# Two heads' inverses stacked on their rows, and the right sides of a chunk made block-diagonal

## The chip, the core and the metric

The kernel runs on one core of one Trainium2 chip. The metric is the device time of one execution in microseconds; three executions of the kernel before took 3189.84 to 3195.04 us, with a median of 3192.13 us. The core has five engines that run their own instruction streams and wait for each other through semaphores: TensorE (PE, with its weight loads shown as PEld), VectorE (DVE), ScalarE (ACT), GpSimd (POOL) and SyncE (SP), which issues the DMAs.

## What is computed

One layer of a hybrid decoder, for a prompt of 2048 tokens and for 8 short sequences of 4 tokens each: a root-mean-square norm, one wide projection, a gated short convolution, an RWKV-7 branch of 16 heads of 64 channels, two output projections merged by gates, one more projection, and a final norm. The change lies in the RWKV-7 recurrence:

```python
def _rwkv7_scan(S0, r, k, v, decay, kk, a):
    def step(S, inp):
        r_t, k_t, v_t, d_t, kk_t, a_t = inp
        sa = jnp.einsum('bhvk,bhk->bhv', S, -kk_t)
        S = (S * d_t[:, :, None, :] + sa[..., None] * (kk_t * a_t)[:, :, None, :]
             + v_t[..., None] * k_t[:, :, None, :])
        y = jnp.einsum('bhvk,bhk->bhv', S, r_t)
        return S, y
```

## The kernel before

**Tiles and stages.** The prompt is cut into four sets of 512 tokens. For each set the first phase projects the normalised rows: every block of 128 output columns is a run of 24 matmuls of 128x512 into a PSUM tile `ip`, eight slices of the contraction by three products of high and low parts (`whl` are the weights, XH and XL the rows). Among these, PE gets the small matmuls of the RWKV branch. The last set is longer by the 32 tokens of the short sequences. A second phase does the output projections; the change does not touch it.

**The recurrence in chunks.** Heads are handled in pairs, eight pairs to a set, each pair on 128 partitions (head 0 on 0 to 63, head 1 on 64 to 127). A set has eight chunks of 64 tokens. Inside a chunk the recurrence is a unit lower triangular system. `rwkv_solve` and `rwkv_merge` invert it for all chunks of a pair ahead of time: DVE inverts 32x32 blocks, ACT copies them from `Xo` into `Xbd` (lines 986 to 988), and two rounds of 32x32 matmuls fill in the off-diagonal blocks. In `Xbd` each chunk has a block-diagonal 128x128 matrix, head 0's inverse at the upper left, head 1's at the lower right, zeros elsewhere.

**The chain.** `rwkv_chain` then goes through the eight chunks of a pair in order, since each needs the state S left by the one before:

1. PE multiplies S by the chunk's keys and receptances into PSUM (`pa`, line 1108).
2. DVE adds `P1` to the two 64x64 blocks of `pa`, giving the right sides `us`, head 0 on partitions 0 to 63, head 1 on 64 to 127, both in columns 0 to 63 (lines 1109 to 1111). ACT scales the state by the chunk's decay (`sp`, line 1113).
3. `inner` (lines 1067 to 1071): PE multiplies `us` by the chunk's matrix in `Xbd`, a 128x64 result in PSUM (`pb`). The next product needs both heads side by side on partitions 0 to 63 of SV. So DVE copies `pb`'s partitions 0 to 63 to SV's columns 0 to 63, and ACT copies `pb`'s partitions 64 to 127 to columns 64 to 127.
4. PE multiplies SV by `BKt` into the other half of `pb` (line 1118), and DVE updates S from it, one instruction per head (lines 1119 to 1121).

There are 4 sets x 8 pairs x 8 chunks = 256 such chunks. Every matmul on f32 tiles is two instructions (two passes) on PE, so the matmul of step 3 counts 512. The short sequences of the last set run through `inner` once per pair as well, from `rwkv_sequences`, with a matrix of their own in slot NCH of `Xbd` (line 1014).

**What sets the order.** The program is recorded once. The `ip` matmuls are the main stream; the RWKV steps are generators that hand control back at each `yield`. `Clock` keeps a planned time for each engine and each tile region, with a cost for each instruction in `Traced.cost` (for ACT 200 + 0.84 ns a column, for DVE 150 + 1.05 ns a column) and a lag of 60 ns to other engines, 200 ns behind PE. A generator goes on when the planned time of PE has reached the planned time at which the regions named in its last `yield` are ready (`Side.run`, line 329). So the planned costs set how many `ip` matmuls stand between two steps of the chain. On the chip each engine then runs its instructions in the recorded order, whatever their real times are.

`us` is a tile of a pool with two buffers (`sm`). `rst`, 1 within a chunk and 0 at its start, is an input of DVE's scan in `rwkv_keys` (line 851), one scan of 512 columns for a pair.

Of the kernel before, what the change touches and what calls it, by code (L numbers as in the profile page):

```python
# [7 lines left out]
F32 = mybir.dt.float32  # L8
F32R = mybir.dt.float32r
BF16 = mybir.dt.bfloat16  # L10
AF = mybir.ActivationFunctionType
ALU = mybir.AluOpType
# [4 lines left out]
P = 128  # L17
# [4 lines left out]
NCH = 8  # L22
NT = NCH * C
# [156 lines left out]
def hybrid_kernel(tc, x_prompt, x_sample, state_conv, state_shift, state_rwkv, norm_g, w_in, conv_w,  # L180
# [219 lines left out]
    con = ph1.enter_context(tc.tile_pool(name="con", bufs=1))  # L400
    xp = ph1.enter_context(tc.tile_pool(name="xp", bufs=1))
# [14 lines left out]
    BKt = xp.tile([P, NC1, P], F32, name="BKt")  # L416
    GMB = [xp.tile([P, NC1, 2, 2, C], F32, name=f"GM{i}") for i in range(2)]
    XB = [xp.tile([P, NC1, P], F32, name=f"Xbd{i}") for i in range(2)]
    SV = xp.tile([P, NC1, P], F32, name="SV")
    early = {}  # L420

# [65 lines left out]
                        base=0, channel_multiplier=1)  # L487
    V.transpose(X0.rearrange("p a b -> p (a b)"), xo0.rearrange("p a b c -> p (a b c)"))

    rst = con.tile([P, NT], F32, name="rst")  # L490
    V.memset(rst, 1.0)
    V.memset(rst.rearrange("p (c t) -> p c t", t=C)[:, :, 0:1], 0.0)
    rst_s = con.tile([P, NSAMP], F32, name="rst_s")
# [314 lines left out]
    def rwkv_keys(th, p, o):  # L808
# [116 lines left out]

        o.update(sz=sz, vT=vT, AR=AR, pe=pe, bv=bv)

    blk = [(slice(64 * h + 32 * b, 64 * h + 32 * b + 32)) for h in range(2) for b in range(2)]

    def rwkv_solve(th, p, o):  # L930
# [50 lines left out]
    def rwkv_merge(th, p, o):  # L981

        GM, Xo, Mo = (o[k] for k in ("GM", "Xo", "Mo"))
        Xbd = o["Xbd"] = XB[(th * NB + p) % 2]
        samp = th == LAST
        for i, g in enumerate(blk):
            A.copy(Xbd[g, 0:NCH, g].rearrange("p c (a e) -> p c a e", e=4),
                                                 Xo[g].rearrange("p a e c -> p c a e"))

        T11 = rw.tile([P, NCH, 32], F32, name="T11")  # L990
        for h in range(2):
            V.transpose(T11[blk[2 * h]], Xbd[blk[2 * h], 0:NCH, blk[2 * h]])
        yield W["bt"], [T11[0:96], Mo[64:96]], 1
        Wm = rw.tile([P, NCH, 32], F32, name="Wm")
        pt = new_pt([P, 512], F32, name="pt")
        for c in range(NCH):
            for h in range(2):
                T.matmul(pt[blk[2 * h + 1], c * 32:(c + 1) * 32], lhsT=Mo[64:96, c, :] if h else GM[0:32, c, 0, 0, 32:64],
                         rhs=T11[blk[2 * h], c, :], start=True, stop=True)
        for h in range(2):  # L1000
            A.copy(Wm[blk[2 * h + 1]], pt[blk[2 * h + 1], 0:NCH * 32].rearrange("p (c t) -> p c t", t=32))
        yield W["bt"], [Wm[32:128], Xbd[32:128]], 1
        pt = new_pt([P, 512], F32, name="pt")
        for c in range(NCH):
            for h in range(2):
                T.matmul(pt[blk[2 * h], c * 32:(c + 1) * 32], lhsT=Wm[blk[2 * h + 1], c, :],
                         rhs=Xbd[blk[2 * h + 1], c, blk[2 * h + 1]], start=True, stop=True)
        for h in range(2):
            A.copy(Xbd[blk[2 * h], 0:NCH, blk[2 * h + 1]],
                   pt[blk[2 * h], 0:NCH * 32].rearrange("p (c t) -> p c t", t=32))  # L1010
        yield W["bt"], (), samp
        if samp:
            for h in range(2):
                V.tensor_copy(Xbd[HS[h], NCH, HS[h]], GM[0:64, NCH, 0, h, :])

            M = Xbd[:, NCH, :]
            pt = new_pt([P, 512], F32, name="pt")
            T.transpose(pt[:, 0:P], M, ident)
            MT = sm.tile([P, P], F32, name="sq")
            A.copy(MT, pt[:, 0:P])  # L1020
            V.tensor_tensor(out=M, in0=M, in1=ident, op=ALU.add)
            yield W["samp"], [M, MT], 1
            for _ in range(SL - 2):
                pt = new_pt([P, 512], F32, name="pt")
                T.matmul(pt[:, 0:P], lhsT=MT, rhs=M, start=True, stop=True)
                V.tensor_tensor(out=M, in0=pt[:, 0:P], in1=ident, op=ALU.add)
                yield W["samp"], [M], 1
        yield W["merge"], [Xbd]
# [38 lines left out]
    def inner(c, pb, us, Xbd):  # L1067

        T.matmul(pb[:, 0:64], lhsT=Xbd[:, c, :], rhs=us, start=True, stop=True)
        V.tensor_copy(SV[0:64, c, 0:64], pb[0:64, 0:64])  # L1070
        A.copy(SV[0:64, c, 64:128], pb[64:128, 0:64])
# [19 lines left out]
    def rwkv_chain(th, p, o):  # L1091

        Yc = y_tile(th, o)
        AR, pe, GM, Xbd = (o[k] for k in ("AR", "pe", "GM", "Xbd"))
        samp = th == LAST
        S = St[p]

        P1 = rw.tile([P, NCH, 64], F32, name="P1")
        yield 0.0, (), 1 + samp
        A.copy(P1.rearrange("p c v -> p (c v)"), own_values(0, NCH, GM))  # L1100
        if samp:
            A.copy(Yc[:, NCH, :], own_values(NCH, 1, GM)[:, 0:64])
        yield W["gk"], [P1]
        for g in range(0, NCH, 4):
            pa = ps_a.tile([P, 4, P], F32, name="pa")
            for c in range(g, g + 4):
                PC = pe[:, c:c + 1]
                T.matmul(pa[:, c - g, :], lhsT=AR[:, c].rearrange("p q t -> p (q t)"), rhs=S, start=True, stop=True)
                us = sm.tile([P, 64], F32, name="us")
                for h in range(2):  # L1110
                    V.tensor_tensor(out=us[HS[h]], in0=pa[0:64, c - g, HS[h]], in1=P1[HS[h], c, :], op=ALU.add)
                sp = sm.tile([P, P], F32, name="sp")
                A.activation(out=sp, in_=S, func=AF.Copy, scale=PC)
                yield W["us"], [us]
                pb = ps_b.tile([P, 2, P], F32, name="pb")
                inner(c, pb[:, 0], us, Xbd)
                yield W["sa"], [SV[0:64, c, :]]
                T.matmul(pb[:, 1, :], lhsT=BKt[:, c, :], rhs=SV[:, c, :], start=True, stop=True)
                for h in range(2):
                    V.scalar_tensor_tensor(out=S[HS[h], HS[h]], in0=pb[HS[h], 1, HS[h]], scalar=PC[HS[h]], in1=sp[HS[h], HS[h]],  # L1120
                                           op0=ALU.mult, op1=ALU.add)
                yield W["state"], [S]
            for h in range(2):
                A.copy(Yc[HS[h], g:g + 4, :], pa[64:128, :, HS[h]])
        yield W["out"], [SV[0:64, 0:NCH]], 1 + samp
        all_rows(o, GM, Yc, samp)
        if samp:
            yield 0.0, (), 1
            pt = new_pt([P, 512], F32, name="pt")
            T.transpose(pt[:, 0:P], S, ident)  # L1130
            so = sm.tile([P, P], F32, name="sq")
            V.tensor_copy(so, pt[:, 0:P])
            for h in range(2):
                SP.dma_start(out=new_rwkv_p[0, 0, 2 * p + h], in_=so[HS[h], HS[h]])
# [261 lines left out]
    ncv = xp.tile([P, NB, 2 + 2 * NS], F32, name="ncv")  # L1396
    xsmp = xp.tile([P, NB, R], F32, name="xsmp")
    scv = xp.tile([P, NB, 2 * NS], F32, name="scv")
    for t in (BK[:, NCH], ARB[0][:, NCH], ARB[1][:, NCH], *XB):
        G.memset(t, 0.0)  # L1400

    def zero_rest():
# [220 lines left out]
```

## Time and profile before

| | |
|---|---|
| median of three executions | 3192.13 us (3189.84 to 3195.04) |
| profiled execution, its own time | 3193.32 us |
| profiled execution, its span from first to last instruction | 3191.6 us |
| mean granted clock of PE | 0.992 |
| DVE, SV<-pb 64x64, 256 copies | 209 ns each |
| ACT, SV<-pb 64x64, 256 copies | 208 ns each |
| first and last matmul pb<-us | 157.1 us and 2641.6 us |

A line of the profile names the engine, the line of the program (here nearly always L121, the helper that records every instruction, so the tile names tell the groups apart), the operation and its tiles as out<-in. In the list of groups come the shape, the count, the busy time in us and the mean length in ns, and behind the second bar the idle time of the engine just before these instructions and what ended it. In the list of waits stand the total in us, the number of times and the longest. In the timeline stand the start in us, the length, the instruction, and in brackets how long its engine had been idle before it. The ends of matmuls are modelled, and the next one starts before the modelled end of the last; distances from start to start are the safer reading.

### The profile page before, as it was taken

How to read it: one execution, taken by the hardware profiler on the slowest of the kernel's cores; microseconds unless marked ns; L12 is line 12 of the kernel's file. 1: busy time of each engine (PE TensorE's matmuls, PEld its weight loads, DVE VectorE, ACT ScalarE, POOL GpSimd, SP SyncE). 2: the span in 40 equal slices, each digit the busy share in tenths (PEclk: the TensorE clock that was granted, in tenths of full speed). 3: DMA queues.
4: the chain of work that ended last, by engine and by line, in shares of the span. 5: the costliest groups of instructions: out<-in, count | busy, mean ns of one | idle time of the engine just before them, and what ended most of it. 6: DMA issues, size and time to landing. Idle time of an engine off the chain costs nothing.

```text
span 3191.6 us, 55625 instructions
## 1 busy us (share of the span) xinstructions
PE 3092.0 (97%) x21530; PEld 2596.5 (81%) x21530; DVE 1992.5 (62%) x5704; ACT 1241.9 (39%) x2571; POOL 309.6 (10%) x517
## 2 busy tenths in 40 slices
PE   7999999999999999999999999999999999999998
PEld 6777777887777778877777789989889889778896
DVE  5687777776666666666666676766677664443332
ACT  5454445444333434434443334344444432211201
POOL 2011111111000001100101010000000000000000
PEclk9999999999999999999999999999999999999999
DMA  8786666644444444444444444434443469988863
GB/s 267 258 267 220 213 212 220 207 173 148 146 162 160 155 159 159 169 157 153 159 153 158 159 147 142 138 127 139 144 143 135 138 223 318 363 337 304 316 241 120
DMA packets 241504, 615.09 MB, mean 193 GB/s; under 512 B 33931, under 2 KB 143620, under 8 KB 187479
## 3 DMA queue, kind: packets, MB, share of 16 engines
q1 hardware_dynamic: 241094, 611.00, 55.8%
q8 instruction: 170, 2.79, 0.4%
q14 instruction: 96, 0.78, 0.1%
q0 software_dynamic: 144, 0.52, 0.0%
HBM read 452.10 MB, written 159.36 MB: 192 GB/s over the span
## 4 chain that ended last, share of the span: by engine, by line
PE 69%; DVE 18%; ACT 5%; issue 5%; DMA 3%; POOL 1%; SPq 0%; ACTq 0%; DVEq 0%; POOLq 0%
PE ip L121 49%; PE pt L121 10%; PE po L121 6%; PE pb L121 3%; DVE X L121 2%; DVE tmp L121 2%; DVE tt L121 2%; ACT tmp L121 2%; DVE Mi L121 2%; DVE whl L121 1%; DVE us L121 1%; PE pa L121 1%; DVE S L121 1%; DMA wraw<-in_w_in_dram 1%; ACT Xbd L121 1%
## 5 line engine op out<-in xcount | busy, mean ns | idle before, releaser
L121 PE MATMUL ip<-XH,whl 128*128 128x512 f32 (+3 forms) x7776 | 2105.1, 351 | 6.6 <-DVE gt L121 3.9
L121 PEld LDWEIGHTS ip<-XH,whl 128*128 128x128 f32 x7776 | 1342.0, 190 | 178.3 <-issue 27.5
L121 PE MATMUL ip<-XL,whl 128*128 128x512 f32 (+3 forms) x3888 | 1364.0, 351 | 2.7 <-POOL XL L121 2.6
L121 PEld LDWEIGHTS ip<-XL,whl 128*128 128x128 f32 x3888 | 738.5, 190 | 79.0 <-issue 7.0
L121 DVE TENSOR_TENSOR X<-X,tt 128x60 f32<-128x60 f32 (+24 forms) x992 | 211.7, 213 | 27.5
L121 DVE TENSOR_TENSOR tt<-Mi,X 128x60 f32<-128x60 f32 (+24 forms) x992 | 209.9, 212 | 27.4
L121 DVE SCALAR_TENSOR_TENSOR S<-pb,pe,sp 64x64 f32<-64x64 f32 x512 | 143.8, 281 | 106.6 <-PE pb L121 100.5
L121 ACT ACTIVATE sp<-S,pe 128x128 f32<-128x128 f32 x256 | 99.5, 400 | 244.7 <-DVE S L121 241.2
L121 ACT ACTIVATE tmp<-ip,vec 128x512 f32<-128x512 f32 (+2 forms) x174 | 103.2, 593 | 231.6 <-PE ip L121 230.2
L121 ACT COPY SV<-pb 64x64 f32<-64x64 f32 x256 | 53.3, 208 | 329.2 <-DVE SV L121 325.5
L121 DVE TENSOR_TENSOR whl<-wraw,whl 128x1024 fp32r<-128x1024 f32 x105 | 134.2, 1279 | 58.0 <-ACT whl L121 57.7
L121 PE MATMUL po<-whl,MH 128*128 128x512 f32 x544 | 170.4, 394 | 0.0
L121 DVE TENSOR_TENSOR us<-pa,P 64x64 f32<-64x64 f32 x512 | 110.2, 215 | 45.2 <-PE pa L121 33.7
L121 PEld LDWEIGHTS pb<-us,Xbd 128*128 128x128 f32 x512 | 85.9, 189 | 56.9 <-PE ip L121 21.5
L121 PE MATMUL ip<-RH,whl 128*128 128x512 f32 (+2 forms) x512 | 128.4, 341 | 1.7 <-DMA whl<-w_or 1.6
L121 PEld LDWEIGHTS pb<-SV,BKt 128*128 128x128 f32 x512 | 85.1, 189 | 54.6 <-ACT SV L121 45.9
L121 ACT CAST whl<-wraw 128x1024 fp32r<-128x1024 f32 x105 | 109.5, 1044 | 50.5 <-DMA wraw<-in_w_out_r_dram 14.8
L121 PE MATMUL pb<-SV,BKt 128*128 128x128 f32 x512 | 107.3, 291 | 17.4 <-ACT SV L121 17.3
L121 DVE TENSOR_TENSOR GM<-pt,mask_p 128x512 f32<-128x512 f32 x128 | 82.4, 685 | 64.4 <-PE pt L121 64.4
L121 PEld LDWEIGHTS po<-whl,MH 128*128 128x128 f32 x544 | 102.2, 188 | 24.0 <-DVE whl L121 0.3
L121 PE MATMUL pb<-us,Xbd 128*128 128x64 f32 x512 | 90.1, 258 | 23.7 <-DVE us L121 23.1
L121 ACT COPY Xbd<-Xo 32x256 f32<-32x256 f32 x128 | 88.1, 688 | 64.0 <-DVE Xo L121 61.9
(494 smaller groups left out, 3838.6 us busy)
## 6 DMA issues: line engine op xcount, KB each, us to landing
wraw<-in_w_in_dram SPq DMA_DIRECT2D x81, 512.0 KB
whl<-w_k SPq DMA_DIRECT2D x24, 1024.0 KB
whl<-w_r SPq DMA_DIRECT2D x24, 1024.0 KB
whl<-w_v SPq DMA_DIRECT2D x24, 1024.0 KB
whl<-w_z SPq DMA_DIRECT2D x24, 1024.0 KB
whl<-w_xin SPq DMA_DIRECT2D x24, 1024.0 KB
whl<-w_cg SPq DMA_DIRECT2D x24, 1024.0 KB
whl<-w_zc SPq DMA_DIRECT2D x24, 1024.0 KB
```

What stands on the lines that cost most here:

```text
L121: r = f(*a, **k)
```

## The change

The two inverses of a chunk are stacked in `Xbd`: both heads write their blocks to columns 0 to 63 (`col` takes the place of `blk` in the column index), head 0 on partitions 0 to 63, head 1 on 64 to 127; columns 64 to 127 of the eight chunks stay zero. The right sides go into a block-diagonal 128x128 tile `UB`, head 1 now in columns 64 to 127; two such tiles, cleared once, take turns. The product then has 128 columns instead of 64, and its partitions 0 to 63 hold both heads side by side, as SV needs them: one ACT copy of 64x128 takes the place of a DVE copy and an ACT copy of 64x64 each. `inner` stays for the short sequences. `rst` becomes bf16, half as large.

```diff
+    UB = [xp.tile([P, P], F32, name=f"UB{i}") for i in range(2)]
...
-    rst = con.tile([P, NT], F32, name="rst")
+    rst = con.tile([P, NT], BF16, name="rst")
...
+    col = [slice(32 * b, 32 * b + 32) for _ in range(2) for b in range(2)]
     blk = [(slice(64 * h + 32 * b, 64 * h + 32 * b + 32)) for h in range(2) for b in range(2)]
...
         for i, g in enumerate(blk):
-            A.copy(Xbd[g, 0:NCH, g].rearrange("p c (a e) -> p c a e", e=4),
+            A.copy(Xbd[g, 0:NCH, col[i]].rearrange("p c (a e) -> p c a e", e=4),
                                                  Xo[g].rearrange("p a e c -> p c a e"))
...
-            V.transpose(T11[blk[2 * h]], Xbd[blk[2 * h], 0:NCH, blk[2 * h]])
+            V.transpose(T11[blk[2 * h]], Xbd[blk[2 * h], 0:NCH, col[0]])
...
-                         rhs=Xbd[blk[2 * h + 1], c, blk[2 * h + 1]], start=True, stop=True)
+                         rhs=Xbd[blk[2 * h + 1], c, col[1]], start=True, stop=True)
         for h in range(2):
-            A.copy(Xbd[blk[2 * h], 0:NCH, blk[2 * h + 1]],
+            A.copy(Xbd[blk[2 * h], 0:NCH, col[1]],
...
-                us = sm.tile([P, 64], F32, name="us")
+                us = UB[c % 2]
                 for h in range(2):
-                    V.tensor_tensor(out=us[HS[h]], in0=pa[0:64, c - g, HS[h]], in1=P1[HS[h], c, :], op=ALU.add)
+                    V.tensor_tensor(out=us[HS[h], HS[h]], in0=pa[0:64, c - g, HS[h]], in1=P1[HS[h], c, :], op=ALU.add)
...
                 pb = ps_b.tile([P, 2, P], F32, name="pb")
-                inner(c, pb[:, 0], us, Xbd)
+
+                T.matmul(pb[:, 0, :], lhsT=Xbd[:, c, :], rhs=us, start=True, stop=True)
+                A.copy(SV[0:64, c, :], pb[0:64, 0, :])
                 yield W["sa"], [SV[0:64, c, :]]
...
-    for t in (BK[:, NCH], ARB[0][:, NCH], ARB[1][:, NCH], *XB):
+    for t in (BK[:, NCH], ARB[0][:, NCH], ARB[1][:, NCH], *XB, *UB):
         G.memset(t, 0.0)
```

The order moves with it, because the planned costs differ. PE, in the second set, fourth pair, third chunk: from the product with the right sides (`pb<-us`, then `pb<-UB`) to the product with SV. Before:

```order
L121 MATMUL pb<-us,Xbd_209 128x64
L121 MATMUL ip<-XH,whl 128x512 x2
L121 MATMUL ip<-XL,whl 128x512
L121 MATMUL ip<-XH,whl 128x512 x2
L121 MATMUL ip<-XL,whl 128x512
L121 MATMUL ip<-XH,whl 128x512 x2
L121 MATMUL ip<-XL,whl 128x512
L121 MATMUL ip<-XH,whl 128x512 x2
L121 MATMUL ip<-XL,whl 128x512
L121 MATMUL ip<-XH,whl 128x512
L121 MATMUL pb<-SV,BKt 128x128
```

and now:

```order
L121 MATMUL pb<-UB_210,Xbd_209 128x128
L121 MATMUL ip<-XH,whl 128x512 x2
L121 MATMUL ip<-XL,whl 128x512
L121 MATMUL ip<-XH,whl 128x512 x2
L121 MATMUL ip<-XL,whl 128x512
L121 MATMUL ip<-XH,whl 128x512
L121 MATMUL pb<-SV,BKt 128x128
```

Thirteen `ip` matmuls stood between the two, seven stand there now. In the chunk behind it (the one whose timeline the prediction quotes) three stand there in both.

DVE, in that next chunk, from the right sides to the next chunk's (the fp32r subtraction is `tmp<-tmp`). Before:

```order
L121 TENSOR_TENSOR us<-pa,P_10297 64x64 x2
L121 TENSOR_TENSOR tmp<-tmp 128x512
L121 COPY SV<-pb 64x64
L121 SCALAR_TENSOR_TENSOR S_474<-pb,pe,sp 64x64 x2
L121 TENSOR_TENSOR bv<-pt,vT 128x512
L121 TENSOR_TENSOR us<-pa,P_10297 64x64 x2
```

and now:

```order
L121 TENSOR_TENSOR UB_211<-pa,P_10125 64x64 x2
L121 SCALAR_TENSOR_TENSOR tmp<-tmp,ip 128x512
L121 TENSOR_TENSOR tmp<-tmp 128x512
L121 SCALAR_TENSOR_TENSOR S_476<-pb,pe,sp 64x64 x2
L121 TENSOR_TENSOR bv<-pt,vT 128x512
L121 TENSOR_TENSOR UB_210<-pa,P_10125 64x64 x2
```

The copy of SV is gone from behind the subtraction; another operation on a gate has moved from ahead of the right sides to behind them.

ACT, same place, from one state copy `sp` to the next. Before:

```order
L121 ACTIVATE sp<-S_474,pe 128x128
L121 ACTIVATE tmp<-ip 128x512
L121 CAST tmp<-tmp 128x512
L121 COPY Yc<-pa 64x256 x2
L121 COPY SV<-pb 64x64
L121 ACTIVATE sp<-S_474,pe 128x128
```

and now:

```order
L121 ACTIVATE sp<-S_476,pe 128x128
L121 COPY Yc<-pa 64x256 x2
L121 ACTIVATE tmp<-ip 128x512
L121 CAST tmp<-tmp 128x512
L121 COPY SV<-pb 64x128
L121 ACTIVATE sp<-S_476,pe 128x128
```

The copy of SV is 64x128 now, and the two copies to `Yc` stand ahead of the gate's ACTIVATE and the CAST instead of behind them.

## The prediction

> **What bounds the kernel now.** I read the page first, then the waits of TensorE (PE), then all waits, then the timeline of one chunk, then the groups of instructions by shape.
>
> ```profile
> span 3191.6 us, 55625 instructions
> PE 3092.0 (97%) x21530; PEld 2596.5 (81%) x21530; DVE 1992.5 (62%) x5704; ACT 1241.9 (39%) x2571; POOL 309.6 (10%) x517
> PE 69%; DVE 18%; ACT 5%; issue 5%; DMA 3%; POOL 1%; SPq 0%; ACTq 0%; DVEq 0%; POOLq 0%
> ```
>
> PE is busy for 97% of the span and carries 69% of the chain that ended last; the change takes no matmul away, so it can only win back time in which PE waits. The waits of PE alone (total us, times, longest) show what there is to win:
>
> ```profile
> PE pb L121 <- DVE us L121: 23.1, 39, 1.6
> PE pb L121 <- ACT SV L121: 17.3, 29, 1.4
> PE ip L121 <- DVE GM L121: 10.2, 1, 10.2
> ```
>
> Two waits of the chunk chain lead: for `us` (VectorE, DVE) and for SV (ScalarE, ACT), the step that the change rewrites. The third is one wait during the start. In the waits of all engines stand how SV is made, and what the weight loads (PEld) wait for it:
>
> ```profile
> ACT SV L121 <- DVE SV L121: 327.1, 169, 4.9
> ...
> PEld pb L121 <- ACT SV L121: 45.9, 83, 1.6
> ...
> DVE SV L121 <- PE pb L121: 36.2, 46, 2.3
> ```
>
> ACT's half of SV waited for DVE's half 169 times: the two copies that the code writes side by side run one behind the other. The timeline of one chunk (start, length, instruction, idle before it) shows a costly case:
>
> ```profile
> 1015.26 0.60 ACT L121 ACTIVATE tmp<-ip 128x512 f32<-128x512 f32 x1 [0.80 <-PE ip L121]
> ...
> 1015.76 0.61 ACT L121 CAST tmp<-tmp 128x512 fp32r<-128x512 f32 x1
> ...
> 1016.50 0.44 DVE L121 TENSOR_TENSOR us<-pa,P 64x64 f32<-64x64 f32 x2
> 1016.66 1.28 POOL L121 TENSOR_TENSOR cv<-cv,tmp 128x512 f32<-128x512 f32 x1 [12.72 <-DVE tmp L121]
> ...
> 1016.97 1.52 DVE L121 TENSOR_TENSOR tmp<-tmp 128x512 fp32r<-128x512 f32 x1
> 1017.03 0.75 ACT L121 COPY Yc<-pa 64x256 f32<-64x256 f32 x2 [0.66 <-DVE us L121]
> ...
> 1017.16 0.33 PE L121 MATMUL pb<-us,Xbd 128*128 128x64 f32 x2
> ...
> 1017.30 0.48 PE L121 MATMUL ip<-XL,whl 128*128 128x512 f32 x1
> ...
> 1017.62 0.63 PE L121 MATMUL ip<-XH,whl 128*128 128x512 f32 x2
> ...
> 1018.42 0.21 DVE L121 COPY SV<-pb 64x64 f32<-64x64 f32 x1
> 1018.66 0.21 ACT L121 COPY SV<-pb 64x64 f32<-64x64 f32 x1 [0.88 <-DVE SV L121]
> 1018.92 0.30 PEld L121 LDWEIGHTS pb<-SV,BKt 128*128 128x128 f32 x2 [1.10 <-ACT SV L121]
> 1018.92 0.49 PE L121 MATMUL pb<-SV,BKt 128*128 128x128 f32 x2 [0.67 <-ACT SV L121]
> ```
>
> `pb` ended at 1017.49. DVE was in a subtraction of 1.52 us beside GpSimd (POOL), so its copy began 0.93 us later; ACT, free since 1017.78, stood idle until DVE had finished; PE stopped.
>
> **The PE price of the wider matmul.** Before, 64 columns go through per chunk and pass; now 128. Nearby stand both widths between the same neighbours:
>
> ```profile
> 1002.32 0.38 PE L121 MATMUL pa<-S,AR 128*128 128x128 f32 x2
> 1002.46 0.48 PE L121 MATMUL ip<-XL,whl 128*128 128x512 f32 x1
> 1002.77 0.62 PE L121 MATMUL ip<-XH,whl 128*128 128x512 f32 x2
> 1003.24 0.40 PE L121 MATMUL ip<-XL,whl 128*128 128x512 f32 x1
> 1003.47 0.63 PE L121 MATMUL ip<-XH,whl 128*128 128x512 f32 x2
> 1003.94 0.33 PE L121 MATMUL pb<-us,Xbd 128*128 128x64 f32 x2
> 1004.08 0.48 PE L121 MATMUL ip<-XL,whl 128*128 128x512 f32 x1
> 1004.40 0.62 PE L121 MATMUL ip<-XH,whl 128*128 128x512 f32 x2
> ```
>
> From the start of the pair to the start of the second group behind it: 0.45 us with 128 columns (1002.32 to 1002.77), 0.46 with 64 (1003.94 to 1004.40). The weights are 128x128 in both, and the stream is paced there by something that the columns don't change. I take **0** where PE runs on. The result does come 0.05 us later (0.38 against 0.33), and where PE has been stopped that shows: 39 waits x 0.03 to 0.05, **+1 us**. The far bound is the difference of the mean durations of the two groups by shape, 291 - 258 = 33 ns, times 512 = 17 us:
>
> ```profile
> L121 PE MATMUL pb<-SV,BKt 128*128 128x128 f32 x512 | 107.3, 291 | 17.4 <-ACT SV L121 17.3
> L121 PE MATMUL pb<-us,Xbd 128*128 128x64 f32 x512 | 90.1, 258 | 23.7 <-DVE us L121 23.1
> L121 DVE COPY SV<-pb 64x64 f32<-64x64 f32 x256 | 53.4, 209 | 37.9 <-PE pb L121 36.2
> L121 ACT COPY SV<-pb 64x64 f32<-64x64 f32 x256 | 53.3, 208 | 329.2 <-DVE SV L121 325.5
> L121 ACT COPY Yc<-pa 64x256 f32<-64x256 f32 x128 | 47.1, 368 | 61.3 <-DVE us L121 60.3
> L121 DVE TENSOR_TENSOR tmp<-tmp 128x512 fp32r<-128x512 f32 x24 | 28.5, 1188 | 8.6 <-ACT tmp L121 8.2
> L121 DVE TENSOR_TENSOR BK<-tmp 128x512 f32<-128x512 f32 x32 | 22.0, 688 | 0.7
> L121 DVE TENSOR_TENSOR_SCAN tmp<-rst,tmp 128x512 f32<-128x512 f32 x32 | 39.1, 1223 | 8.4 <-ACT tmp L121 8.1
> ```
>
> A rule speaks against the change here: the Trainium skill, "TensorE: Matmul & The Clock Gate", section Back-to-back issue gap, gives about 60 cycles for 1 to 64 columns and 134 for 128, in its isolated figures. By that page the wider matmul would be an estimated 74 cycles or 31 ns longer, 16 us over 512, and would eat the gain; the two 0.45 us rows above don't bear it out. The same section says that a stream of weight loads and matmuls is spaced by both, which agrees with these rows.
>
> **The SV copy.** Removed: 256 DVE copies of 209 ns, 53.4 us of DVE's 1992.5. ACT's copy grows from 64x64 (208 ns) to 64x128; between 208 and 368 ns for 256 columns the slope is 160/192 = 0.83 ns, so 208 + 53 = 261 ns, 14 us more in all on an engine that is idle 61% of the time. From the end of `pb` the old route took 0.21 + 0.03 + 0.21 + 0.05 = 0.50 us (lengths and hand-overs of the chunk above) and DVE's queue on top. The new one takes 0.03 + 0.26 + 0.05 = 0.34, plus 0.05 for the later end of `pb`, and ACT's queue on top. In the old order of the chunk above ACT would copy from 1017.81 to 1018.07 and free PE at 1018.12; a pair of `ip` matmuls takes 0.47 us (1003.47 to 1003.94), so the slot was at 1018.09: a loss of 0.03 instead of 0.83. The new order puts the copies to Yc, the gate's ACTIVATE and the CAST ahead of the copy, and ten `ip` matmuls instead of six between `pa` and `pb`. From the start of `pa`: `pa` 0.38, `us` 0.04 + 0.44, the three ACT steps 0.09 + 0.75 + 0.60 + 0.61 make 2.9 us; `pb` starts at 0.14 + 10 x 0.233 = 2.5 and ends at 2.9 too, the copy is through at 3.2, the slot is at 2.5 + 0.14 + 3 x 0.233 = 3.3. No loss, if DVE takes `us` at once.
>
> How much is that in all? The old loss per case, 0.83, is 0.16 more than PE's idle time and 0.27 less than PEld's. So the 29 idle waits of PE cost 17.3 + 29 x 0.16 = 22 us; the 54 others, in PEld's row alone, add little. I take **25 us**, with 17 and 46 (the two rows as they stand) as bounds. Nearly half of it is the case above: the fp32r subtraction comes once in each pair of the first three sets (24) and averages 1188 ns where a like one takes 688, so 24 x 0.50 = 12 us. In the order of the built program the chunk of that case keeps its three `ip` matmuls between `pb` and the next matmul, so all 12 go. Of the other 13 I count half, 6. Against that, the planner trusts the shorter route: counted along PE's order, 117 of 256 chunks have over a quarter of a microsecond less other work between the two matmuls, 27 have more, and the rest are as before. Where ACT is late there, a new stall comes; I charge 3. Sum for SV: **-15 us**.
>
> **The other edits.** The waits for `us`, 23.1 + 39 x 0.16 = 29 us by the same conversion, hang on DVE; its two adds keep their shape, and a DVE queue lighter by 2.7% gives **-1**, with +10 and -14 as ends, since every order changes a little. The scan reads `rst` in bf16: no row has a bf16 input on DVE; between half of its 39.1 us and as much again the price is on DVE, which waits inside the keys steps hide; I take 0, nearest to its own row (1223 ns). The stacked columns of Xbd leave every copy, transpose and 32x32 matmul of the merge at its shape: 0. Two more memsets of POOL at setup cost 0.22 us each by the row below, long ahead of the first `pb`: 0. A smaller pool moves no queue; no DMA is added or moved.
>
> ```profile
> L121 POOL MEMSET SV<- x1: 222/222/222, 11.7 to 11.7; 128x128 f32 x1
> ```
>
> **Sum.** 0 + 1 - 15 - 1 = -15 us. The profiled execution took 3193.3 us (span 3191.6), 1.2 above the median of the three runs: 3178 on its scale, **3177** on the median's.
>
> **The rivals.**
> - *The wait only moves.* DVE stays as late as it is, and what SV no longer loses is lost one step on, at `us` or the state. For it: `us` is the larger PE wait, and the long DVE instructions remain. Against it: behind the SV copy of the example DVE waited 0.82 us for PE, which absorbs lateness. Gain 3 us: 3189. Chance 0.12.
> - *The wider matmul costs its columns.* Price 17 us by the difference of means: 3177 + 17 - 1 = 3193. The 0.45 us rows speak against it; this is also what the skill's table would give. Chance 0.08.
> - *Slower: ACT's queue takes DVE's place, at shorter distances.* Three `ip` matmuls leave 0.14 + 3 x 0.23 = 0.83 us from the start of `pb`; the copy needs 0.38 + 0.34 = 0.72. A copy behind a weight cast of 1044 ns waits half of that on average, 0.52, and stops PE for 0.41. From 15/0.41 = 37 such chunks on the gain is gone; with 80 of the 117 it is 80 x 0.41 - 15 = +18: 3210. For it: the planner cut the mean distance from 1.81 to 1.33 us, more than the 0.11 us that the route itself saves. Against it: ACT is busy 39%, DVE 62%. Chance 0.11.
>
> ```profile
> L121 ACT CAST whl<-wraw 128x1024 fp32r<-128x1024 f32 x105 | 109.5, 1044 | 50.5 <-DMA wraw<-in_w_out_r_dram 14.8 <-DMA wraw<-in_w_in_dram 11.8 <-PE ip L121 9.6
> ```
>
> - *More than forecast.* All 25 us go, and half of the 29 at `us`, because DVE is never blocked by a copy that waits for PE (36.2 us above): -39, 3153. Chance 0.14.
> - That the change doesn't do what it says is excluded by the order: one ACT copy of 64x128, no DVE copy.
>
> **How the numbers follow.** Forecast 3177, chance 0.55, own range 3168 to 3185. A measurement of this kernel tells about 0.2%, 6 us, from no change. Faster: 0.55 + 0.14 = 0.69; same: 0.12 + 0.08 = 0.20; slower: 0.11. The range of 8 in 10 goes from 3154, nearly all of the best case, to 3196, past the two cases without a change; it leaves out the slow case and the edge of the best.
>
> **What would show it.** SV's row: ACT copies of 64x128 near 261 ns, released by PE and no longer by DVE; PE's wait for ACT SV down from 17.3 to 5 to 8 us. The wide matmul: 0.45 to 0.46 us from its start to the second group behind it; if 0.5 or more, the second rival holds. `us`: 23.1 us of PE idle, give or take 10; a rise by 12 is the first rival. New PE waits for SV behind weight casts would be the third.

## The result, and the profile after

The changed kernel is slower by 26 us: 3218.18 us (3216.42 to 3218.99, 5 runs) against 3192.13 us (3186.25 to 3195.15, 5 runs), a ratio of 1.0082 with a 95% interval of 1.0068 to 1.0095. The forecast was 3177, and the range ended at 3196.

The page of after, span and busy times:

```profile
span 3216.5 us, 55431 instructions
PE 3098.4 (96%) x21530; PEld 2599.6 (81%) x21530; DVE 1963.8 (61%) x5448; ACT 1247.6 (39%) x2571; POOL 303.5 (9%) x519
```

The waits of after (total us, times, longest), those of PE first, in their order:

```profile
PE pb L121 <- DVE UB L121: 19.7, 52, 1.3
PE pa L121 <- DVE S L121: 12.8, 23, 2.3
PE ip L121 <- DVE GM L121: 10.5, 1, 10.5
PE pt L121 <- DVE Yc L121: 8.7, 8, 1.7
PE ip L121 <- DVE gt L121: 5.8, 1, 5.8
PE pt L121 <- ACT SV L121: 4.9, 5, 1.1
PE pt L121 <- DVE us L121: 4.7, 5, 1.5
...
PE pb L121 <- ACT SV L121: 3.8, 8, 1.1
```

```profile
ACT SV L121 <- PE pb L121: 295.9, 155, 5.9
...
PEld pa L121 <- DVE S L121: 33.5, 52, 2.7
PEld pb L121 <- ACT SV L121: 14.2, 29, 1.5
```

PE's wait for SV fell from 17.3 to 3.8 us, and ACT's copy is now released by PE and no longer by DVE. New rows stand beside it: `pa` for the state S (12.8; 1.9 before), and the tile `pt` for Yc, the tile of a pair's outputs (8.7; 0.6 before), and for SV (4.9; none before). The two rows of before:

```profile
PE pa L121 <- DVE S L121: 1.9, 3, 0.9
...
PE pt L121 <- DVE Yc L121: 0.6, 2, 0.4
```

`pt` is not a step of the chunk chain: these are two PSUM tiles that the keys, solve, merge, load, output and sequence steps share.

The groups of after by shape (busy, mean ns, idle before) that the change touches:

```profile
L121 PE MATMUL pb<-UB,Xbd 128*128 128x128 f32 x512 | 106.2, 289 | 20.5 <-DVE UB L121 19.7
L121 ACT COPY SV<-pb 64x128 f32<-64x128 f32 x256 | 65.6, 256 | 298.3 <-PE pb L121 295.9
L121 DVE TENSOR_TENSOR_SCAN tmp<-rst,tmp 128x512 f32<-128x512 bf16 x32 | 39.1, 1223 | 25.3 <-ACT tmp L121 25.1
```

PE's waits alone do not add up to the loss: a step may also come late behind its weight load, which has waits of its own. A safer account charges each PE instruction with the distance from the start of the one before it to its own start, and adds these up by step. It adds up to the span to within 0.5 us. Against before, in us:

| step | after | run 1 below (old order) |
|---|---|---|
| product with SV | -26.1 | -32 |
| product with S (`pa`) | +19.2 | +19.5 |
| product with the right sides and the main matmuls (`pb<-UB` and `ip`) | +7 | +1 |
| all `pt` steps | +23.7 | +1.8 |
| sum, with small rest | +25 | -10 |

And by place, counted along the `ip` and `po` matmuls on the weights `whl`, whose sequence is the same in all kernels: up to the 1700th (first set) +12.7, up to the 6300th (the sets between) -2.5, from there on (last set, transition, second phase) +15.1. Of the 23.7 us at `pt`, 12.7 fall in the first part and 11.2 in the last.

### The profile page after: what moved, and what is told of

Read it like the earlier page. It is cut to its first block, busy times and chain, and to the rows that moved or that the text cites. A ratio compares the mean times of both kernels' runs of the same rounds, so it can differ in the third digit from the quotient of the medians.

```text
span 3216.5 us, 55431 instructions
## 1 busy us (share of the span) xinstructions
PE 3098.4 (96%) x21530; PEld 2599.6 (81%) x21530; DVE 1963.8 (61%) x5448; ACT 1247.6 (39%) x2571; POOL 303.5 (9%) x519
## 5 line engine op out<-in xcount | busy, mean ns | idle before, releaser
L121 ACT COPY SV<-pb 64x128 f32<-64x128 f32 x256 | 65.6, 256 | 298.3 <-PE pb L121 295.9
L121 DVE TENSOR_TENSOR UB<-pa,P 64x64 f32<-64x64 f32 x512 | 110.2, 215 | 59.5 <-PE pa L121 49.7
L121 PEld LDWEIGHTS pb<-UB,Xbd 128*128 128x128 f32 x512 | 84.8, 189 | 61.5 <-PE ip L121 33.0
L121 PE MATMUL pb<-UB,Xbd 128*128 128x128 f32 x512 | 106.2, 289 | 20.5 <-DVE UB L121 19.7
L121 PEld LDWEIGHTS pa<-S,AR 128*128 128x128 f32 x512 | 87.1, 188 | 45.2 <-DVE S L121 33.5
L121 PE MATMUL pa<-S,AR 128*128 128x128 f32 x512 | 104.3, 285 | 14.9 <-DVE S L121 12.8
```

The costliest lines, as they stand in the source:

```text
L121: r = f(*a, **k)
```

## The experiments

### Is it the instructions or the order?

**Run 1** has after's instructions, but the planner is told of the two old copies. On PE 17648 of 17882 instructions stand where before has them.

```diff
-                A.copy(SV[0:64, c, :], pb[0:64, 0, :])
+                nc.scalar.copy(SV[0:64, c, :], pb[0:64, 0, :])
+                clock.add("DVE", [SV[0:64, c, 0:64]], [pb[0:64, 0, 0:64]], 150 + 1.05 * 64)
+                clock.add("ACT", [SV[0:64, c, 64:128]], [pb[64:128, 0, 0:64]], 200 + 0.84 * 64)
```

> The changed kernel, but the planner is told of the two old copies (DVE 217 ns, ACT 254 ns) in place of the one ACT copy; 17648 of PE's 17882 matmul instructions then stand where they stood before the change. Theory A (the planner's tighter distances cost the time, the new instructions save it): PE's wait for SV falls as in the changed kernel (near 4 us of idle), its wait for S at pa stays near 2 us, and the time is 3165 to 3180. Rival B (the new instructions themselves cost: the wider matmul, the block-diagonal right sides, the longer ACT copy): 3205 to 3220, as the changed kernel.

Measured: 3183.74 us (3178.48 to 3187.63), ratio 0.9976 (0.9967 to 0.9986). **Run 2** is the reverse: before's instructions, and the planner is told of one ACT copy; 17378 places are after's.

```diff
-                inner(c, pb[:, 0], us, Xbd)
+                T.matmul(pb[:, 0, 0:64], lhsT=Xbd[:, c, :], rhs=us, start=True, stop=True)
+                nc.vector.tensor_copy(SV[0:64, c, 0:64], pb[0:64, 0, 0:64])
+                nc.scalar.copy(SV[0:64, c, 64:128], pb[64:128, 0, 0:64])
+                clock.add("ACT", [SV[0:64, c, :]], [pb[0:64, 0, :]], 200 + 0.84 * 128)
```

> The kernel before, but the planner is told of one ACT copy of 64x128 where the two old copies run; 17378 of PE's 17882 matmul instructions then stand where the changed kernel has them. Theory A: the short distances meet the long old route, PE waits more for SV than before (30 us of idle or more), and the time is 3225 or more. Rival B: about 3192, as before.

Measured: 3219.22 us (3212.72 to 3221.55), ratio 1.0084 (1.0067 to 1.0101). So the whole loss comes with the order: the new order costs 28 us with the old instructions and 34 with the new; the new instructions gain 7 us in the old order (3183.74 against 3191.12, the median of before measured beside it). The PE waits of run 1, its first two rows:

```profile
PE pb L121 <- DVE UB L121: 21.7, 41, 1.6
PE pa L121 <- DVE S L121: 13.1, 26, 1.9
```

The wait for SV is gone (0.3 us are left), but S at `pa` now stops PE for 13.1 us: over half of what the faster copy saves is lost one step on (from start to start 19.5 of 32 us).

Theory A was right that the order costs the time, and wrong in how. It put run 1 at 3165 to 3180 with `pa` near 2 us, and run 2 at 3225 or more with 30 us of idle at SV. In run 2 PE waits no longer for SV than before:

```profile
PE pb L121 <- ACT SV L1118: 17.3, 31, 1.5
```

So the shorter distances do not lose their time at SV. From start to start run 2 loses 11.9 us at the `pt` steps, 9.3 at `pb<-us` and the `ip` matmuls, and 4.9 at the product with SV.

**Run 3**: the wide matmul alone. SV is copied by DVE and ACT, 64x64 each, both from partitions 0 to 63 now; before's order.

```diff
-                A.copy(SV[0:64, c, :], pb[0:64, 0, :])
+                V.tensor_copy(SV[0:64, c, 0:64], pb[0:64, 0, 0:64])
+                A.copy(SV[0:64, c, 64:128], pb[0:64, 0, 64:128])
```

> The changed kernel with its wide matmul and block-diagonal right sides, but SV is again made by a DVE copy and an ACT copy of 64x64 each, both from partitions 0 to 63; PE's order is that of before to 17713 of 17882 places. If the wider matmul costs PE nothing, the time is 3187 to 3198; if it costs its columns (33 ns more on 512 instructions), 3205 to 3212.

Measured: 3195.01 us (3188.71 to 3199.11), ratio 1.0011 (1.0002 to 1.002). The width costs 1 to 6 us, not 17.

### Is it the shorter distance from pb to SV?

**Run 4** is after, with 217 ns of DVE's planned time taken up in each chunk, as the old copy did; **run 5** is after, with SV planned to be ready 480 ns later.

```diff
                 A.copy(SV[0:64, c, :], pb[0:64, 0, :])
+                clock.t["DVE"] += 150 + 1.05 * 64
```

```diff
-                A.copy(SV[0:64, c, :], pb[0:64, 0, :])
+                nc.scalar.copy(SV[0:64, c, :], pb[0:64, 0, :])
+                clock.add("ACT", [SV[0:64, c, :]], [pb[0:64, 0, :]], 200 + 0.84 * 128, 60.0 + 480.0)
```

> The changed kernel; the planner reserves 217 ns a chunk on DVE, as for the old copy, without letting SV wait for it. Mean other work between the two matmuls of a chunk 1.38 us (1.33 in the changed kernel, 1.78 under the old plan). Theory A1 (the shortened distance at SV is what costs): 3210 to 3220, no better than the changed kernel. Theory A2 (DVE's plan lost 217 ns a chunk that DVE needs elsewhere): 3180 to 3195. Theory A3 (the loss comes from any order away from the one that the planner's tables fit, wherever it differs): between 3195 and 3220, with no relation to the distance.

> The changed kernel; the planner takes SV to be ready 480 ns later, nothing is reserved on DVE. Mean other work between the two matmuls of a chunk 1.59 us. A1: 3180 to 3195. A2: 3210 to 3220. A3: between 3195 and 3220.

Measured: 3208.99 us (ratio 1.0055, 1.004 to 1.007) with a mean distance of 1.38 us, and 3205.69 us (1.0045, 1.003 to 1.006) with 1.59 us. They give back 9 and 12 of the 34 us, where A3 had them, though run 5 has gone half of the way back to the old distance (1.33 in after, 1.81 before). **Runs 6 and 7** plan the state update at 281 instead of 217 ns, nearer to what the trace shows, once in after and once in run 1:

```diff
             per = {"transpose": 1.6, "tensor_tensor_scan": 2.1}.get(op, 1.05)
+            if op == "scalar_tensor_tensor" and n == 64:
+                per += 1.0
```

> The changed kernel; the planner takes DVE's state update for 281 ns, as the trace has it, instead of 217. Distance at SV 1.35 us. If the wait for S at pa (12.8 us of idle in the changed kernel) comes from this cost alone, it falls to 2 to 6 us and the time to 3200 to 3208. A1 and A3: 3210 to 3225.

> New instructions under the old plan as in the first run, with the state update at 281 ns in the plan. If the wait for S at pa (13.1 us in that run) comes from this cost, the time falls from 3184 to 3170 to 3178. A3: at or above 3190, since the order moves again.

Measured: 3220.72 us (1.0092, 1.0075 to 1.0109) and 3204.38 us (1.0042, 1.0027 to 1.0057). Run 7 keeps the old distance (in the trace 2.18 us in the mean from the start of `pb<-UB` to the product with SV; 2.15 in run 1, 1.72 in after), has a truer cost, and loses 21 us against run 1. The truer cost did not shorten the time in either run, as it would have if the wait at `pa` came from it. So neither the distance nor the old copies' planned time is the cause: an order that moves away from before's comes out 13 to 30 us above before (runs 2, 4 to 7 and after), whichever cost moves it.

### Where does the moved order lose?

The account by place shows the same in all six moved orders so far: loss in the first set (3 to 17 us) and from the last set on (5 to 28), none or a gain in the sets between, but for 0.6 us in run 5. (Where exactly the line between the sets is drawn moves a single number by up to 5 us, in runs 4 and 5 above all; the pattern stays.) Four runs switch the planner's account of SV by set (`th`); the condition is the only thing that differs, but in run 11, which also plans the state update at 281 ns in the sets between.

```diff
+                nc.scalar.copy(SV[0:64, c, :], pb[0:64, 0, :])
+                if th == 0:
+                    clock.add("DVE", [SV[0:64, c, 0:64]], [pb[0:64, 0, 0:64]], 150 + 1.05 * 64)
+                    clock.add("ACT", [SV[0:64, c, 64:128]], [pb[64:128, 0, 0:64]], 200 + 0.84 * 64)
+                else:
+                    clock.add("ACT", [SV[0:64, c, :]], [pb[0:64, 0, :]], 200 + 0.84 * 128)
```

Run 8, as above (`th == 0`):

> The new instructions; in the first set the planner is told of the two old copies, in the other three sets of the one new copy. On PE the first set then stands in before's order (all places within one ip matmul) and everything from the second half of the second set on in after's. Theory (the loss sits in certain stages, each by itself: from start to start, after lost 12.7 us in the first set where the new instructions in the old order gained 5.5): the first set's 18 us come back and the rest stays: 3218 - 18 = 3200, with set 0 within 2 us of the old-order run. First rival (the loss comes from the shorter distance from pb to SV, 27 + 7 = 34 us over four sets alike): only a quarter comes back, 3209. Second rival (what is lost early is made up later, so that only the total can be read): 3215 or more.

Run 9, `th in (0, LAST)`:

> The new instructions; the planner is told of the two old copies in the first and the last set, of the new copy in the two between. The first set stands in before's order; the last set stands in a third order (a tenth to a third of its places are those of before, as few those of after), since it starts from a shifted state. Theory (any order of the last set other than before's costs there: the six displaced orders so far lost 6 to 28 us from the last set's first chunk to the last chain, 15 in the mean): 3184 + 4 in the middle sets + 6 to 20 = 3194 to 3208. Rival (the shorter distance costs, and the last set has the old distance here): half of 34 comes back, 3218 - 17 = 3201, but with the last set within 3 us of the old-order run. Rival (the last set costs only what the planner's account of SV costs it): 3184 to 3190.

Run 10, `th < LAST`:

> The new instructions; the planner is told of the two old copies in the first three sets and of the one new copy in the last. On PE the first three sets stand in before's order to the place, the last set in an order of its own. Theory (the last set's displacement costs there, by itself): nothing before the last set, 6 to 28 us in it: 3190 to 3212, likeliest 3199. First rival (shorter distance, a quarter of 34): 3192. Second rival (a displaced last set costs nothing unless it starts displaced): 3184.

Run 11, `th in (0, LAST)`, and the true state cost between:

> The new instructions; the planner is told of the two old copies in the first and the last set, and in the two middle sets of the one new copy and of a state update of 281 ns instead of 217. On PE the first set stands in before's order to the place, the last set in before's order too (99% of its chunk steps within one ip matmul), and only the middle sets in a new one. Theory (loss only where the first and the last set are displaced; in the middle sets the run with the true state cost stood 8 us below the old-order run): 3184 - 8 = 3176, at least not above 3187. Rival (shorter distance costs everywhere; half of the chunks have it here): 3184 + 17 = 3201.

| run | first set | between | last set on | median, us | ratio (95%) |
|---|---|---|---|---|---|
| after | moved, +12.7 | moved, -2.5 | moved, +15.1 | 3218.18 | 1.0082 (1.0068 to 1.0095) |
| 1 | old, -5.5 | old, -5.3 | old, +1.1 | 3183.74 | 0.9976 (0.9967 to 0.9986) |
| 8 | old, -6.4 | moved, -2.3 | moved, +17.2 | 3200.52 | 1.0031 (1.0018 to 1.0043) |
| 9 | old, -3.3 | moved, -3.2 | third order, +22.6 | 3206.84 | 1.0049 (1.0035 to 1.0062) |
| 10 | old, -3.3 | old, -6.6 | third order, +15.8 | 3194.45 | 1.0008 (0.9999 to 1.0017) |
| 11 | old, -5.9 | moved, -5.0 | old, +0.6 | 3185.36 | 0.9981 (0.9972 to 0.999) |

(The three columns in the middle are differences of one profile each; the first set, in the same order in runs 8 to 10, differs by 3 us between profiles, which is how far such a number can be trusted.) Run 8 came out at the forecast 3200. Run 10's total cannot tell the forecast 3199 from the first rival's 3192; its loss does lie in the last set. Run 11, whose sets between have the shorter distance, lies with run 1: the rival that charges the distance, 3201, falls. Its forecast of 3176 was 9 us too low, though, since the 8 us looked for in the sets between did not come (-5.0 against -5.3 in run 1). Run 9's last set is planned with the old copies and still loses 23 us, since it starts from a shifted state and never gets back to before's order.

### What does PE wait for there?

The timeline of after, where the sixth pair of the first set is prepared while the fifth is finished, with the `ip` matmuls and the rows of other steps left out. PE transposes the sixth pair's BK, its keys, into two `pt` tiles:

```profile
526.27 1.15 PE L121 MATMUL pt<-SV,GM 128*64 128x64 f32 x32
...
527.35 0.66 PE L121 MATMUL pt<-ident,vT 128*128 128x128 f32 x4
...
528.28 0.45 DVE L121 STREAM_TRANSPOSE Xo<-X 128x256 f32<-128x256 f32 x1
528.76 2.68 ACT L121 COPY Xbd<-Xo 32x256 f32<-32x256 f32 x4 [3.50 <-DVE Xo L121]
529.44 0.43 DVE L121 STREAM_TRANSPOSE T<-Xbd 32x256 f32<-32x256 f32 x1 [0.71 <-ACT Xbd L121]
529.90 0.69 DVE L121 TENSOR_TENSOR Yc<-pt,Yc 128x512 f32<-128x512 f32 x1
530.65 0.42 PEld L121 LDWEIGHTS pt<-ident,BK 128*128 128x128 f32 x4 [2.15 <-DVE Yc L121]
530.65 0.66 PE L121 MATMUL pt<-ident,BK 128*128 128x128 f32 x4 [1.72 <-DVE Yc L121]
...
531.45 1.17 ACT L121 COPY SV<-pt 64x512 f32<-64x512 f32 x2
...
532.67 0.66 PE L121 MATMUL pt<-ident,BK 128*128 128x128 f32 x4 [1.13 <-ACT SV L121]
```

The transposes need nothing from Yc or SV: they wait until the two tiles have been read, one by DVE's addition to Yc, the other by ACT's copy to SV. DVE's addition stands behind a transpose that waits for ACT, and ACT's copy behind four copies of the sixth pair's inverses. PE loses 1.72 + 1.13 us. In run 8, whose first set has the old order, the same steps (timeline, same place) meet no such queue, and PE does not stop:

```profile
522.49 1.15 PE L121 MATMUL pt<-SV,GM 128*64 128x64 f32 x32
...
523.69 0.69 DVE L121 TENSOR_TENSOR Yc<-pt,Yc 128x512 f32<-128x512 f32 x1 [1.20 <-PE pt L121]
524.26 1.18 ACT L121 COPY SV<-pt 64x512 f32<-64x512 f32 x2 [2.28 <-PE pt L121]
...
524.53 0.60 PE L121 MATMUL pt<-ident,BK 128*128 128x128 f32 x4
...
525.49 0.66 PE L121 MATMUL pt<-ident,BK 128*128 128x128 f32 x4
```

There the merge ran earlier; DVE and ACT were idle and waiting for PE.

**Run 12** moves the four copies and the transposes behind the two readers, in two pairs, and leaves PE's order alone. The planner is told of the copies where they stood; the instructions are issued later. A dependency holds them there, since the engines' order is not the recorded one to the letter: in after's trace DVE's addition to Yc (529.90) stands between the two transposes T<-Xbd (529.44 and 530.78), which the code records one right behind the other.

```diff
-        for i, g in enumerate(blk):
-            A.copy(Xbd[g, 0:NCH, col[i]].rearrange("p c (a e) -> p c a e", e=4),
-                                                 Xo[g].rearrange("p a e c -> p c a e"))
...
-        for h in range(2):
-            V.transpose(T11[blk[2 * h]], Xbd[blk[2 * h], 0:NCH, col[0]])
+        first(V0, A0)
+        held.append(lambda: first(nc.vector, nc.scalar))
...
+                if r is not None and (th, p) in ((0, 3), (0, 5)):
+                    tc.add_manual_dep(r.ins, loaded[th, p].ins.name, DEP, reason="queue")
```

> After's kernel with PE's order kept (17878 of 17882 places, no matmul further than 8 places), and one thing changed in the queues of ACT and DVE, in two pairs of the first set (its fourth and sixth): ACT's four copies of the inverses into Xbd (2.7 us together) stand behind its copy SV<-pt instead of ahead of it, and DVE's two transposes of Xbd behind its addition to Yc instead of around it. In after's trace PE stops there twice in the sixth pair: 1.7 us for Yc and 1.1 us for SV, since the two pt tiles that the transposes of BK need are still being read. Theory (the first set's loss is made of such places, where steps of three kinds share two pt tiles and the queues of ACT and DVE): at these two places the waits go, some 2.6 us each, PE's waits for Yc up to 570 us fall from 5.1 to about 1.7 us and its pt waits for SV from 3.3 to about 1; the sum is 3213 (3211 to 3215). Rival (PE is stopped at the next step anyway, now for the transposes T that come later): the waits turn up at pt<-T or pt<-Xbd, and the time stays at 3217 to 3219.

Measured: 3217.42 us (3214.91 to 3218.45), ratio 1.0081 (1.0067 to 1.0094): the total lies in the rival's range, 0.8 us under after, and cannot tell the two apart, as 4 us is its interval. The timeline at the same place:

```profile
530.92 0.69 DVE L121 TENSOR_TENSOR Yc<-pt,Yc 128x512 f32<-128x512 f32 x1
...
531.34 1.17 ACT L121 COPY SV<-pt 64x512 f32<-64x512 f32 x2
...
531.67 0.65 PE L121 MATMUL pt<-ident,BK 128*128 128x128 f32 x4 [0.58 <-DVE Yc L121]
...
532.57 0.66 PE L121 MATMUL pt<-ident,BK 128*128 128x128 f32 x4 [0.24 <-ACT SV L121]
```

The waits fell from 2.85 to 0.82 us here. Counted along the main matmuls, PE gained 1.8 to 2.0 us for good at each of the two places and lost nothing behind them, as the theory said against the rival; its size was 2.6. In that one profile a delay of over 3 us ahead of both places, where nothing had been changed, hid it in the span.

**Runs 13 to 16** ask the same of all places at once. One tile `pa` is given up for a third tile `pt`; the planner goes on reckoning with two, so PE's order stays (17713 of 17882 places in run 14). Runs 13 and 15 give up the `pa` tile alone.

```diff
-    ps_t = ph1.enter_context(tc.tile_pool(name="ps_t", bufs=2, space=PSUM))
-    ps_a = ph1.enter_context(tc.tile_pool(name="ps_a", bufs=2, space=PSUM))
+    ps_t = ph1.enter_context(tc.tile_pool(name="ps_t", bufs=3, space=PSUM))
+    ps_a = ph1.enter_context(tc.tile_pool(name="ps_a", bufs=1, space=PSUM))
```

After, one `pa`; and with three `pt`:

> After with one PSUM tile pa instead of two (to make room for the next run); every engine's order is after's to the place. Control. The first matmul of every second group of four chunks now waits until the copies to Yc have read the tile: 64 such places, and the copies stand 0.7 to 1.5 us behind the right sides. Expected by both theories: 3218 to 3228, the loss at pa.

> The same with three PSUM tiles pt instead of two, the planner still reckoning with two; PE's order is after's in 17713 of 17882 places. Theory (the steps wait for a pt tile to be read out): most of the loss at the pt steps goes, 10 to 18 us less than x13. Rival (they wait for their inputs, which stand in the queues of DVE and ACT): within 4 us of x13.

Run 1, one `pa`; and with three `pt`:

> The new instructions in the old order (3184), with one tile pa; every engine's order is that run's to the place. Control: 3184 to 3194 by both theories.

> The same with three tiles pt, the planner still reckoning with two. The old order loses little at the pt steps, so the ring is not what it waits for: theory 0 to 4 us less than x15. Rival: within 4 us too. If it comes out more than 8 us under x15, the ring costs in every order and does not explain the difference between them.

| run | order | pt tiles | median, us | ratio (95%) | pt steps against before | last set on |
|---|---|---|---|---|---|---|
| 13 | after's | 2 | 3222.63 | 1.0092 (1.0075 to 1.0108) | +23.3 | +15.2 |
| 14 | after's | 3 | 3202.14 | 1.0031 (1.0019 to 1.0042) | +4.2 | +16.0 |
| 15 | old | 2 | 3181.89 | 0.9966 (0.9953 to 0.9979) | +1.5 | -1.1 |
| 16 | old | 3 | 3178.40 | 0.9956 (0.9941 to 0.997) | -7.8 | +1.1 |

Giving up a `pa` tile cost nothing that the runs can tell: run 15 came out 2 us under its range, and run 13, 4 us above after with overlapping intervals, shows no loss at `pa` (+19.5 us from start to start, +19.2 in after). In after's order the third tile takes 20 us off the median, more than the 10 to 18 forecast, and 12 off the profiled span (3216.6 to 3204.5); run 13's profile was at the fast end of its runs, run 14's at the slow end. At the `pt` steps it takes off 19.1. In the old order it takes off 9.3 us at the `pt` steps, of which 4.4 come back in the chunk chain, and 3.5 us of the median, which the intervals do not tell from nothing. In run 14 the place shown above reads (timeline):

```profile
522.05 2.69 ACT L121 COPY Xbd<-Xo 32x256 f32<-32x256 f32 x4 [3.50 <-DVE Xo L121]
522.16 0.60 PE L121 MATMUL pt<-ident,BK 128*128 128x128 f32 x4
...
523.21 0.69 DVE L121 TENSOR_TENSOR Yc<-pt,Yc 128x512 f32<-128x512 f32 x1
...
523.96 0.66 PE L121 MATMUL pt<-ident,BK 128*128 128x128 f32 x4 [1.20 <-DVE Yc L121]
```

DVE and ACT are queued as before, but the first transposes have a free tile, and the second ones wait for the first reader instead of the second: the same row of waiting, shifted by one tile. At this place that is a ring too short, not an input that is late. The Trainium skill, "Perfetto Trace Analysis", section Optimization Strategy, says that the same gap repeating on the engine that should be full can mean that there isn't enough PSUM for the next tile; at these steps the runs agree, by 19.1 us.

How much of the order's cost is the ring? The third tile helps in both orders, so only the difference counts. With two tiles the moved order stands 40.7 us above the old one (run 13 against run 15), with three still 23.7 (run 14 against run 16). So the ring explains some 17 of 41 us by the medians, and 9 of 37 by the four profiled spans; at the `pt` steps themselves the gap goes from 21.8 to 12.0 us. It is a part of the cause, and the smaller one. (Over 8 us in the old order was to be the sign that the ring does not explain the difference; the median of run 16 stays under it, its `pt` steps in the one profile do not.)

What is left, 28 us between the profiles of runs 14 and 16, lies in the first set (12) and from the last set on (15). Run 14 still loses 16 us against before from the last set on, although the `pt` steps there went from +11.3 to +4.7. Two parts show as rows: PE's wait for `gt`, a gate, at the transition to the second phase (5.9 us in run 14, 3.0 in run 16), and its wait for `us` in the steps of the short sequences (4.7 against 1.4). The rest is spread over many places, and its cause stays open.

Run 16 is the fastest version found, 14 us below before. Against run 1 (3183.74) its gain comes from the `pa` and `pt` tiles together, and the intervals of runs 1, 15 and 16 overlap.

## Why the prediction was wrong, step by step

- **The wide matmul at 0 (bounds 0 and 17): right.** In after's timeline the stretch from its start to the second group behind it is again 0.45 us (1017.85 to 1018.30 and 1011.51 to 1011.96), and run 3 puts the whole price at 1 to 6 us. By the isolated gap of the Trainium skill, "TensorE: Matmul & The Clock Gate", section Back-to-back issue gap, it would have been an estimated 16; run 3 speaks against that, and agrees with the same section's sentence on a stream paced by loads and matmuls together.

```profile
1017.85 0.38 PE L121 MATMUL pb<-UB,Xbd 128*128 128x128 f32 x2
1017.99 0.48 PE L121 MATMUL ip<-XL,whl 128*128 128x512 f32 x1
1018.30 0.62 PE L121 MATMUL ip<-XH,whl 128*128 128x512 f32 x2
```

- **The SV copy at -15: right in kind, too small.** The copy takes 256 ns (261 forecast), PE's wait fell to 3.8 us (5 to 8 forecast), and from start to start the step gained 26 us in after and 32 in run 1. The chunk that the prediction worked out by hand lies at 1027.62 in after (other rows left out):

```profile
1027.62 0.38 PE L121 MATMUL pa<-S,AR 128*128 128x128 f32 x2
...
1030.17 0.38 PE L121 MATMUL pb<-UB,Xbd 128*128 128x128 f32 x2
1030.31 0.48 PE L121 MATMUL ip<-XL,whl 128*128 128x512 f32 x1
...
1030.60 0.26 ACT L121 COPY SV<-pb 64x128 f32<-64x128 f32 x1
1030.63 0.63 PE L121 MATMUL ip<-XH,whl 128*128 128x512 f32 x2
...
1031.10 0.38 PE L121 MATMUL pb<-SV,BKt 128*128 128x128 f32 x2
```

  From the start of `pa`, `pb` starts after 2.55 us (2.5 forecast), the copy is through after 3.24 (3.2), and PE takes the product after 3.48 (3.3) without a stop. The working held in its own example.
- **`us` at -1: right.** The idle row went from 23.1 to 19.7 us (21.7 in run 1). In the account from start to start `pb<-UB` costs 15 us more and the `ip` matmuls 9 to 14 less, since the second pass of the wide matmul begins 109 ns behind the first instead of 55, and the `ip` matmul behind it sooner by about as much.
- **Not in the sum: S at `pa`.** The wait turned up there in both orders (1.9 to 13.1 us in run 1, +19.5 us from start to start). The first rival had this mechanism ("what SV no longer loses is lost one step on, at `us` or the state"), at a gain of 3; with the old order the gain is 7.4, between that and the 15 of the forecast.
- **The step that failed: the charge of 3 us for the moved order.** The text counted what the planner's new times did to one distance, `pb` to SV ("117 of 256 chunks"), and priced only that. The order costs 28 us with the old instructions and 34 with the new. Most of it lies at steps that the change doesn't touch: of the 35 us between the profiles of after and run 1, 22 stand at the transposes, scores and merges that pass through the two `pt` tiles, nearly all in the first and the last set, and 6 at the product with SV. (In run 2, with the old instructions, the `pt` steps carry 12 of 28.) At the place followed above, and at a second one like it, the moved order had put merge copies ahead of the readers of `pt` in the queues of ACT and DVE. That all of the `pt` loss comes about so is not shown: the third tile takes back 9 to 17 us of the order's cost, and the cause of the rest stays open. The rows of ACT shown with the change, the copies to Yc now ahead of the gate, were read only for what they do to SV.
- **The third rival** had the sign and, with 3210, nearly the size, but its mechanism is not what happened: it put new stalls at SV behind weight casts, and PE's wait for SV is down to 3.8 us; runs 2, 5, 7 and 11 rule out the distance as the main price. That its number came near is luck. Its own evidence, the cut from 1.81 to 1.33 us, was a sign of a moved order and not the cost.
- **rst in bf16 at 0: right;** the scan took 39.1 us before and after. The merge and the memsets were not measured by themselves; run 1 carries them and is faster than before.
- Why the planner misplaces these steps was not tried. It does track when a `pt` tile comes free, but by planned times; it plans the four copies to Xbd at 4 x 415 = 1.66 us, and they take 2.68.

## What to carry to other kernels

A change that alters what a planner or scheduler is told has two parts, and they can be measured apart: the new instructions in the old order, and the old instructions in the new order. Here the first gained 7 us and the second lost 28. When the order moves, price the steps that the change does not name as well, above all those that share a small ring of tiles: look for who reads each tile and what stands ahead of that reader in its queue. A wait "for Yc" or "for SV" at an instruction that uses neither is a wait for a buffer, and one more buffer in an unchanged order is the test, if the same buffer is tried in the old order as well.

## What the runs showed of the hardware that was not expected

- A 128-column f32 matmul in a stream of 512-column ones takes no longer from its start to the second group behind it than a 64-column one (0.45 and 0.46 us in the rows shown; medians of 0.457 in after and 0.454 before over the 77 and 89 places with an XL and then an XH group behind it), and only its own two passes are further apart (109 against 55 ns): over 512 instructions 1 to 6 us.
- Giving up one of two `pa` tiles cost nothing that can be measured (run 15 against run 1: 3181.89 and 3183.74 us; run 13 against after: 3222.63 and 3218.18 us, with ratios to before whose intervals overlap).
- DVE's and ACT's copy of SV never ran side by side, neither when they read different halves of the partitions nor when both read the same 64: in before, run 2 and run 3, ACT's copy starts at least 32 ns behind the end of DVE's in all 256 chunks, and the profile puts the wait down to DVE's copy. Whether that comes from the tile both read or from the tile both write was not tried.

```profile
ACT SV L121 <- DVE SV L121: 348.5, 177, 4.9
```
